# The second group's recurrence of a hybrid decoder step: 64-token chunks and one shared function

## The chip, the cores and the metric

The kernel runs on one core of one Trainium2 chip. The metric is device microseconds of one execution. TensorE (PE) multiplies, VectorE (DVE), ScalarE (ACT) and GpSimd (POOL) do elementwise work, SyncE (SP) issues transfers. Each engine works through its own queue in order and waits on semaphores for the others.

## What is computed

Two layers of a hybrid decoder step over 1024 prompt tokens and 8 single-token decodes. A layer projects the normalized input once, and from that feeds an HGRN2 group (6 heads, key width 64), a GLA group (6 heads, key width 32, value width 64) and an S5 group, each with a gate; an output projection follows. HGRN2 and GLA share one recurrence with a decay for each key channel:

```
S_t = diag(a_t) S_{t-1} + k_t v_t^T ;  o_t = S_t^T q_t
```

computed by chunks of tokens:

```python
b = jnp.cumsum(gc, axis=1)
o_inter = jnp.einsum('bthk,bhkv->bthv', qc * jnp.exp(b), S)
...
att = jnp.einsum('bthk,bshk,btshk->bths', qc, kc, decay)
o_intra = jnp.einsum('bths,bshv->bthv', att, vc)
...
S_new = jnp.exp(b_last)[..., None] * S + jnp.einsum(
    'bshk,bshv->bhkv', kc * jnp.exp(b_last[:, None] - b), vc)
```

The chunk's length is free: any length gives the same outputs up to rounding.

## The kernel before

All is fp32. The trunk of a layer is its in-projection: 25 weight tiles of 128 columns, each multiplied with 1032 tokens. Weights and activations are split into a high and a low part, and three products are summed into the PSUM tile ps_g; these matmuls of 384 or 264 columns are called gemms here (line 156 is the helper that issues every matmul). A tile's result is evicted by DVE at line 737. Between gemms the kernel advances Python generators, its "threads": one for S5, one for each unit of the recurrences, for the decodes and the gates. tick() moves every thread one yield further, twice per 24 gemms. So a yield places what follows it some gemms later in the program, and a scheduler then fixes the in-order queue of each engine. A lock lets one recurrence run at a time; need() waits for free slots in SBUF. PSUM has two banks each for ps_g, for ps_o and for ps_aux, and ps_att spans two.

A unit of the HGRN2 group, called A below (unit_a, five lines up to 1100), takes two heads of width 64, which fill 128 partitions; there are three in a layer. A tile of the GLA group, called B (unit_b, lines 1103 to 1202), takes heads of width 32: four in the first tile (128 partitions), two in the second (64). Two heads make one unit of output, so B has three such units in a layer too. Both go through the same steps:

- decay (line 867): running sums of the log decay, one DVE scan for each chunk, then their middle value is taken off. A has chunks of 64 tokens, 16 scans; B of 128, 8 scans.
- transposes of the keys into ktm (A) or ktmB (B), by PE, evicted by ACT.
- factors (line 886): GpSimd writes a chunk's decay to every state column in the tile Sp.
- kv: k^T v of each chunk on PE into ps_aux; DVE multiplies by the decay (line 1032 in A, twice; 1144 in B, once).
- states (line 891): one DVE scan along Sp and the products (in the tile onorm) makes the state of every chunk.
- att: keys by queries into ps_att. A's small matmul is 64 by 64, B's 128 by 128 with 32 rows for the contraction.
- mask: DVE copies the part below the diagonal into the zeroed tiles atts (line 1064 with maskA, line 1166 with maskB).
- inter: state by query into ps_o; intra: masked block by value, summed into the same bank.
- headnorm (lines 893 to 910): normalizes ps_o into onorm; sl is its subtraction at line 901, two PE matmuls follow.

In A the masks of a unit are bound to stand behind its inter matmuls ("behind", line 1064), one yield before intra, and a unit covers all 1024 tokens with two ps_o banks. In B a unit goes in two halves of 512 tokens; a half's inter and intra stand together, and the next half's query-key product and masks are issued behind them, ahead of headnorm.

Of the kernel before, what the change touches and what calls it, by code (L numbers as in the profile page):

```python
# [14 lines left out]
P = 128  # L15
# [23 lines left out]
def tile_hybrid_step(ctx: ExitStack, tc: tile.TileContext, a: dict, nl=NL, limit=RANGE):  # L39
# [105 lines left out]
    def act(out, in_, func, **kw):  # L145
        return S.activation(out=out, in_=in_, func=func, **kw)  # L146
# [20 lines left out]
    maskB = cst.tile([P, P], I8, name="maskB")  # L167
# [487 lines left out]
    def layer(l, slow=False):  # L655
# [296 lines left out]


# [8 lines left out]
        def unit_a(j, s1, s2, qs):  # L962
# [41 lines left out]
            kt, qt = s2, qs  # L1004
            yield from core_lock.take()
            yield from need(1)
            ktm = alloc("ktm", [P, 8, P])
            for h in range(2):
                p = psum("aux")
                for i in range(4):  # L1010
                    t0 = 512 * h + P * i
                    TE.transpose(out=p[:, i * P:(i + 1) * P], in_=kt[:, t0:t0 + P], identity=ident)
                act(out=ktm[:, 4 * h:4 * h + 4, :].rearrange("p a b -> p (a b)"), in_=p, func=AF.Copy)
                yield
            Sp = tmp("Sp", [P, 1024])
            factors(Sp, ac, 16)
            S3 = Sp.rearrange("p (v c) -> p c v", c=16)
            yield from need(1)
            on = alloc("onorm", [P, NT])
            po = None  # L1020
            asb = {}

            def kv():
                p = [psum("aux").rearrange("p (c v) -> p c v", v=64) for _ in range(2)]
                for c in range(16):
                    pr_, par = divmod(c, 2)
                    for h in range(2):
                        mm(p[par][64 * h:64 * h + 64, pr_, :], ktm[64 * par:64 * par + 64, pr_, 64 * h:64 * h + 64],
                           vA[64 * par:64 * par + 64, pr_, (2 * j + h) * 64:(2 * j + h) * 64 + 64])
                x = on[:, :T].rearrange("p (v k r) -> p r k v", k=8, r=2)  # L1030
                for par in range(2):
                    V.tensor_tensor(out=x[:, par], in0=p[par], in1=ac.rearrange("p (k r) -> p r k", r=2)[:, par]
                                    .unsqueeze(2).to_broadcast([P, 8, 64]), op=ALU.mult)
                states(Sp, on, 16)


            da = [x.rearrange("p a b c -> p (a b c)").rearrange("p (h a t) -> p h a t", h=2, t=64) for x in atts]

            def att():
                p = psum("att", (P, 2, 512))  # L1040
                for pair in range(8):
                    for par in range(2):
                        t0 = (2 * pair + par) * 64
                        for h in range(2):
                            mm(p[64 * par:64 * par + 64, h, pair * 64:pair * 64 + 64], kt[64 * h:64 * h + 64, t0:t0 + 64],
                               qt[64 * h:64 * h + 64, t0:t0 + 64])
                return p

            def inter(po):

                for pair in range(8):
                    for par in range(2):
                        c = 2 * pair + par
                        for h in range(2):
                            ph = slice(64 * h, 64 * h + 64)
                            if c:
                                x = mm(po[par][ph, pair * 64:pair * 64 + 64], S3[ph, c - 1, :], qt[ph, c * 64:c * 64 + 64],
                                       start=(pair == 1 - par), stop=False)
                                if pair == 7:
                                    yield x  # L1060

            def mask(p, done):
                for i, d in enumerate(da):
                    x = V.copy_predicated(out=d, mask=maskA.unsqueeze(1).unsqueeze(1).to_broadcast([P, 2, 4, 64]),
                                          data=p[:, :, 256 * i:256 * i + 256].rearrange("p h (a t) -> p h a t", t=64))
                    behind(x, done)

            def intra(po):

                for pair in range(8):  # L1070
                    for par in range(2):
                        r = slice(64 * par, 64 * par + 64)
                        for h in range(2):
                            mm(po[par][64 * h:64 * h + 64, pair * 64:pair * 64 + 64],
                               vA[r, pair, (2 * j + h) * 64:(2 * j + h) * 64 + 64], da[pair // 4][r, h, pair % 4, :],
                               start=False, stop=(pair == 7))

            if j == 0:
                for x in atts:
                    G.memset(x, 0.0)  # L1080
            kv()
            p = att()
            yield
            yield
            onorm[j] = on
            po = [psum("o") for _ in range(2)]
            mask(p, list(inter(po)))
            release(ktm)
            sfin = tmp("sfin", [P, 64], bufs=2)
            G.tensor_copy(out=sfin, in_=S3[:, 15])  # L1090
            SY.dma_start(out=a["hg_p"][l, :, j], in_=sfin)
            yield
            intra(po)
            release(kt)
            release(qt)
            x = on[:, :T].rearrange("p (c r t) -> p r c t", r=2, t=64)
            for par in range(2):
                yield from headnorm(po[par], x[:, par], 64)
                yield
            core_lock.give()  # L1100


        def unit_b(ti, s, q, k):
# [12 lines left out]
            ac = yield from decay(s[:, :T], s[:, :T], pr, P, 1.0 / 16.0)  # L1116
# [7 lines left out]
            yield from core_lock.take()  # L1124
            yield from need(1)
            ktm = alloc("ktmB", [P, 8, pr])
            for h in range(2):
                p = psum("aux")
                for i in range(4):
                    t0 = 512 * h + P * i  # L1130
                    TE.transpose(out=p[:, i * pr:(i + 1) * pr], in_=k[:pr, t0:t0 + P], identity=ident[:pr, :pr])
                act(out=ktm[:, 4 * h:4 * h + 4, :].rearrange("p a b -> p (a b)"), in_=p[:, :4 * pr], func=AF.Copy)
                yield
            Sp = tmp("Sp", [P, 1024])[:pr]
            factors(Sp, ac, 8)
            S3 = Sp[:, :512].rearrange("p (v c) -> p c v", c=8)
            yield from need(1)
            on = alloc("onorm", [P, NT])
            p = psum("aux").rearrange("p (c v) -> p c v", v=64)
            for c in range(8):  # L1140
                for h in range(nh):
                    mm(p[32 * h:32 * h + 32, c, :], ktm[:, c, 32 * h:32 * h + 32],
                       vB[:, c, (h0 + h) * 64:(h0 + h) * 64 + 64])
# [471 lines left out]
```

## Time and profile before

| | before |
|---|---|
| runs, us | 1102.15, 1095.07, 1093.75 (median 1095.07) |
| profiled execution, us | 1096.44 |
| its span, us | 1094.5 |
| mean granted clock of TensorE | 0.963 of full speed |
| PE busy | 1023.2 us, 8071 instructions |
| DVE busy | 696.4 us |
| ACT, POOL busy | 483.7 us, 463.7 us |

The span runs from the first to the last instruction of the core. One fp32 matmul of the program appears as two instructions in the trace. Small matmuls on different parts of the array overlap, so a group's mean duration says little of its cost: the busy time divided by the count does, as overlap is counted once in it. Idle time of an engine is given with what ended it.

### The profile page before, as it was taken

The numbers are of one execution on the slowest core, as the hardware profiler recorded it, in microseconds if no ns is written. First come the engines' busy times: TensorE is split into PE (matmuls) and PEld (weight loads), VectorE is DVE, ScalarE is ACT, GpSimd is POOL, SyncE is SP. The second block draws the span as 40 slices with busy tenths as digits, with TensorE's granted clock in tenths as the row PEclk, the third lists the DMA queues.
The fourth block names the chain that finished last, engine by engine and source line by source line (L and its number), as shares of the span: only waits on it lengthen the run. The fifth ranks groups of instructions, "written<-read, shape, count | busy, mean of one in ns | idle before, by whom it ended". The sixth has DMA issues, their size and how long they took to land.

```text
span 1094.5 us, 21166 instructions
## 1 busy us (share of the span) xinstructions
PE 1023.2 (93%) x8071; PEld 956.4 (87%) x8071; DVE 696.4 (64%) x1591; ACT 483.7 (44%) x996; POOL 463.7 (42%) x619
## 2 busy tenths in 40 slices
PE   6899999999989899999999998999998999999992
PEld 5789977789889789999999987878997889999992
DVE  8996844955776798544574574482468685652344
ACT  8233223355533646643332412334553555763431
POOL 4536673413553644522172277340244253561323
PEclk8999969999989899999999999999998989999996
DMA  7131112211112021144414113111111112112314
GB/s 226 55 99 51 42 55 76 61 51 40 61 36 61 29 89 40 39 143 129 124 53 127 48 38 98 52 48 50 29 54 47 56 39 80 39 57 87 100 53 145
DMA packets 78812, 76.78 MB, mean 70 GB/s; under 512 B 24524, under 2 KB 60652, under 8 KB 78700
## 3 DMA queue, kind: packets, MB, share of 16 engines
q1 hardware_dynamic: 78700, 75.33, 22.8%
q8 instruction: 65, 1.06, 0.4%
q14 instruction: 47, 0.39, 0.1%
HBM read 58.01 MB, written 15.53 MB: 67 GB/s over the span
## 4 chain that ended last, share of the span: by engine, by line
PE 60%; DVE 21%; POOL 6%; issue 3%; DMA 3%; ACT 3%; SPq 2%; DVEq 0%; POOLq 0%; ACTq 0%
PE ps_g L156 47%; PE ps_aux L156 7%; PE ps_o L156 4%; PE ps_att L156 1%; DMA x<-in_xT 1%; DVE wl L289 1%; DVE ep L867 1%; DVE sB L867 1%; DVE s5W L581 1%; DVE sl L901 1%; DVE Sp L891 1%; SPq L638 1%; ACT ep L146 1%; DVE flags L337 1%; PE ps_aux L846 1%
## 5 line engine op out<-in xcount | busy, mean ns | idle before, releaser
L156 PE MATMUL ps_g<-hh,wh 128*128 128x384 f32 (+1 forms) x1168 | 386.4, 331 | 9.1 <-DVE z L737 3.0
L156 PE MATMUL ps_g<-hh,wl 128*128 128x384 f32 (+1 forms) x1168 | 384.0, 329 | 2.0 <-POOL wl L289 1.5
L156 PE MATMUL ps_g<-lo,wh 128*128 128x384 f32 (+1 forms) x1168 | 382.3, 327 | 0.0
L156 PEld LDWEIGHTS ps_g<-hh,wh 128*128 128x128 f32 x1168 | 224.9, 193 | 15.8 <-DVE z L737 3.8
L156 PEld LDWEIGHTS ps_g<-hh,wl 128*128 128x128 f32 x1168 | 224.1, 192 | 6.8 <-POOL wl L289 2.2
L156 PEld LDWEIGHTS ps_g<-lo,wh 128*128 128x128 f32 x1168 | 224.8, 192 | 2.8 <-issue 0.6
L289 POOL TENSOR_TENSOR wl<-raw,wh 128x256 fp32r<-128x256 f32 x127 | 108.3, 854 | 255.5 <-ACT wh L146 219.2
L146 ACT ACTIVATE wh<-raw 128x256 fp32r<-128x256 f32 x258 | 102.4, 411 | 123.4 <-PE ps_g L156 106.2
L156 PE MATMUL ps_g<-m,wh 128*128 128x384 f32 (+1 forms) x567 | 136.2, 320 | 0.0
L289 DVE TENSOR_TENSOR wl<-raw,wh 128x256 fp32r<-128x256 f32 x131 | 77.6, 592 | 41.0 <-ACT wh L146 32.9
L156 PEld LDWEIGHTS ps_g<-m,wh 128*128 128x128 f32 x567 | 99.0, 188 | 0.4
L156 PE MATMUL ps_g<-m,wl 128*128 128x384 f32 (+1 forms) x261 | 83.4, 319 | 0.0
L1333 POOL TENSOR_TENSOR z<-z,sg 128x384 f32<-128x384 f32 (+1 forms) x48 | 48.5, 1011 | 50.9 <-ACT sg L146 40.1
L156 PEld LDWEIGHTS ps_g<-m,wl 128*128 128x128 f32 x261 | 49.1, 188 | 0.2
L146 ACT ACTIVATE sg<-z 128x384 f32<-128x384 f32 (+1 forms) x48 | 23.4, 487 | 35.9 <-DVE z L1331 30.5
L1343 DVE SCALAR_TENSOR_TENSOR onorm<-z,vec,onorm 128x384 f32<-128x384 f32 (+1 forms) x36 | 23.4, 650 | 20.6 <-POOL z L1333 20.6
L156 PE MATMUL ps_g<-vx,wh 128*128 128x384 f32 (+1 forms) x129 | 34.0, 321 | 0.0
L737 DVE TENSOR_TENSOR z<-ps_g,rn 128x384 f32<-128x384 f32 (+1 forms) x48 | 24.4, 507 | 14.0 <-PE ps_g L156 14.0
L146 ACT ACTIVATE sg<-sg 128x384 f32<-128x384 f32 (+2 forms) x56 | 31.8, 568 | 3.2 <-DVE sg L774 2.2
L146 ACT ACTIVATE sg<-sg,ones 128x384 f32<-128x384 f32 (+2 forms) x52 | 32.3, 622 | 0.9
L1422 DVE TENSOR_TENSOR ext<-ps_g,ext 128x384 f32<-128x384 f32 (+1 forms) x24 | 12.3, 512 | 31.9 <-PE ps_g L156 31.9
L1422 DVE TENSOR_TENSOR lo<-ps_g,ext 128x384 f32<-128x384 f32 (+1 forms) x24 | 12.3, 512 | 30.7 <-PE ps_g L156 30.6
(404 smaller groups left out, 1926.7 us busy)
## 6 DMA issues: line engine op xcount, KB each, us to landing
raw<-in_wf SPq DMA_DIRECT2D x100, 256.0 KB, 2.8
raw<-in_wo SPq DMA_DIRECT2D x32, 256.0 KB, 2.8
x<-in_xT SPq DMA_DIRECT2D x16, 192.0 KB, 4.7
ext<-in_xT SPq DMA_DIRECT2D x16, 192.0 KB, 2.4
x1d<-ext SPq DMA_DIRECT2D x16, 192.0 KB, 2.2
ext<-x1d SPq DMA_DIRECT2D x16, 192.0 KB, 3.2
usd<-ucp SPq DMA_DIRECT2D x4, 512.0 KB, 3.3
s5U<-usd SPq DMA_DIRECT2D x32, 64.0 KB, 2.4
```

Of the source, the lines that this page charges most:

```text
L146: return S.activation(out=out, in_=in_, func=func, **kw)
L156: return TE.matmul(out=out, lhsT=lhsT, rhs=rhs, start=start, stop=stop)
L289: e.tensor_tensor(out=wl, in0=r, in1=wh.bitcast(F32), op=ALU.subtract)
L337: V.tensor_reduce(out=flags[:p0, c:c + 1], in_=x2d, axis=mybir.AxisListType.X, op=ALU.min)
L581: V.tensor_tensor_scan(out=W_[:, ri, q], data0=m8[:, q0 + q:q0 + q + 1].to_broadcast([P, P]), data1=W_[:, ri, q], initial=0.0, op0=ALU.mul ...
L638: SY.dma_start(out=yk[16 * g:16 * g + 16, :T].rearrange("p (t k) -> p t k", t=8), in_=ysd[:, :, g, :].rearrange("t c k -> c t k"))
L737: V.tensor_tensor(out=dst[:, o:o + n], in0=p, in1=rn[:, o:o + n], op=ALU.mult)
L846: TE.transpose(out=p[:, c * P:(c + 1) * P], in_=f[:, t0:t0 + P], identity=ident)
L867: V.tensor_tensor_scan(out=g[:, cs], data0=zero[:pr].to_broadcast([pr, ch]) if plus is None else plus[:, cs], data1=x[:, cs], initial=0.0, ...
L1333: G.tensor_tensor(out=z[:, c], in0=z[:, c], in1=sg[:, c], op=ALU.mult)
L1343: V.scalar_tensor_tensor(out=on[:, c], in0=z[:, c], scalar=g, in1=on[:, c], op0=ALU.mult, op1=ALU.mult)
L1422: V.tensor_tensor(out=x, in0=p, in1=xo, op=ALU.add)
```

## The change

unit_a's recurrence becomes a function, recurrence(pr, kd, kt, qt, ac, vt, h0, fin_out, units), which both groups call: pr partitions, heads of width kd, and a list of the units of two heads that share one kv and one states step. B calls it with kd = 32 and with decays over 64 tokens. So B's chunks are 64 tokens: 16 for a head. A chunk's query-key block is 64 by 64, so the masked blocks of a head cover half the area, and the masks of a unit are two, with maskA, where they were four with maskB. maskB goes, with its load, and so do GpSimd's four memsets of atts (line 1080). Each of B's units now covers 1024 tokens, and its order is A's: query-key, yield, inter and masks behind it, yield, intra, headnorm of either bank with yields.

```diff
-    maskB = cst.tile([P, P], I8, name="maskB")
...
+        def recurrence(pr, kd, kt, qt, ac, vt, h0, fin_out, units):
...
+            Sp = tmp("Sp", [P, 1024])[:pr]
+            factors(Sp, ac, 16)
...
+            def kv():
+                p = [psum("aux").rearrange("p (c v) -> p c v", v=64) for _ in range(2)]
+                for c in range(16):
+                    pair, par = divmod(c, 2)
+                    for h in range(nh):
+                        mm(p[par][kd * h:kd * h + kd, pair, :], ktm[64 * par:64 * par + 64, pair, kd * h:kd * h + kd],
+                           val(par, pair, h))
...
+                states(Sp, on[:pr], 16)
...
+            def att(u):
+                p = psum("att", (P, 2, 512))
+                for pair in range(8):
+                    for par in range(2):
+                        t0 = (2 * pair + par) * 64
+                        for h in range(2):
+                            r = slice((2 * u + h) * kd, (2 * u + h + 1) * kd)
+                            mm(p[64 * par:64 * par + 64, h, pair * 64:pair * 64 + 64], kt[r, t0:t0 + 64], qt[r, t0:t0 + 64])
...
+            kv()
+            p = att(0)
+            yield
+            yield
+            for u, unit in enumerate(units):
+                if u:
+                    yield from need(1)
+                    on = alloc("onorm", [P, NT])
+                    p = att(u)
+                    yield
+                onorm[unit] = on
+                po = [psum("o") for _ in range(2)]
+                mask(p, list(inter(u, po)))
...
+                yield
+                intra(u, po)
...
+                for par in range(2):
+                    yield from headnorm(po[par], x[:, par], 64)
+                    yield
+            core_lock.give()
...
-            if j == 0:
-                for x in atts:
-                    G.memset(x, 0.0)
...
+            yield from recurrence(P, 64, s2, qs, ac, vA, 2 * j, a["hg_p"][l, :, j], [j])
...
-            ac = yield from decay(s[:, :T], s[:, :T], pr, P, 1.0 / 16.0)
+            ac = yield from decay(s[:, :T], s[:, :T], pr, 64, 1.0 / 16.0)
...
+            yield from recurrence(pr, 32, k, q, ac, vB, h0, a[f"gl_p{ti}"][l], [3 + 2 * ti + hp for hp in range(nh // 2)])
...
-        for i, m in enumerate((maskA, maskB, maskD)):
+        for i, m in ((0, maskA), (2, maskD)):
```

The change also moves instructions in the queues. Three places follow.

PE in layer 0 at B's second tile, between its kv (ps_aux from v and ktmB) and its inter (ps_o from qk and Sp); s5V, s5O, s5U and s5T are S5's, ident marks a transpose. Before:

```order
910 L156 MATMUL ps_aux_2494<-v_849,ktmB_2417 32x64 x16
...
924 L156 MATMUL ps_att_2635<-qk_213_1668,kb_214_1669 128x128 x3
925 L156 MATMUL ps_aux_2531<-s5V_2043,s5O_2437 128x136 x2
...
929 L846 MATMUL ps_aux_2557<-ident,vf_2216 128x128 x4
930 L156 MATMUL ps_o_2620<-qk_213_1668,Sp_2490 64x128 x6
```

In the left-out rows stand ten further S5 matmuls and nine gemms. After, at the same place, where wg, yh and yl belong to S5's gate:

```order
1068 L156 MATMUL ps_aux_2723<-v_845,ktm_2643 32x64 x16
1069 L156 MATMUL ps_aux_2724<-v_845,ktm_2643 32x64 x16
1070 L850 MATMUL ps_aux_2793<-ident,vf_2295 8x128
1071 L156 MATMUL ps_aux_2850<-yh_2828,wg_2815 128x384
1072 L156 MATMUL ps_aux_2850<-yl_2829,wg_2815 128x384
...
1077 L156 MATMUL ps_o_2859<-qk_212_1664,Sp_2719 64x64 x2
```

The left-out rows are four more matmuls of the gate. The S5 matmuls and the gemms between kv and inter are gone from this place, and the query-key product stands ahead of kv now (rows 967 to 969, not shown).

DVE in layer 0 at the second unit of B's first tile: its masks (line 1166 before, 1013 after) and S5's block (sd to the scans s5W). Before:

```order
397 L1166 COPY_PREDICATED atts_92<-maskB,ps_att_2158 128x512
398 L1166 COPY_PREDICATED atts_93<-maskB,ps_att_2158 128x512
399 L901 TENSOR_TENSOR sl_2171<-sq_2169,sh_2170 128x512
400 L568 COPY sd_751<-s5V_2043 128x64
401 L571 TENSOR_TENSOR t_83_752<-s5V_2043,s5E_1547 128x512
402 L586 COPY s5V_2043<-x_43_275 128x8x8
403 L592 TENSOR_TENSOR so_282<-so_282,sd_751 128x2x32
404 L910 TENSOR_TENSOR onorm_1884<-ps_o_2141,sq_2210 128x512
405 L575 TENSOR_TENSOR t_83_752<-s5V_2043,s5E_1547 128x512
406 L581 SCALAR_TENSOR_TENSOR s5W_2232<-sm_274,s5W_2232 128x128 x3
407 L1166 COPY_PREDICATED atts_92<-maskB,ps_att_2252 128x512
```

After:

```order
400 L567 COPY sd_747<-s5V_2145 128x64
401 L570 TENSOR_TENSOR t_82_748<-s5V_2145,s5E_1543 128x512
402 L585 COPY s5V_2145<-x_42_271 128x8x8
403 L591 TENSOR_TENSOR so_278<-so_278,sd_747 128x2x32
404 L909 TENSOR_TENSOR onorm_1888<-ps_o_2078,sq_2290 128x8x64
405 L574 TENSOR_TENSOR t_82_748<-s5V_2145,s5E_1543 128x512
406 L580 SCALAR_TENSOR_TENSOR s5W_2311<-sm_270,s5W_2311 128x128 x4
407 L584 MEMSET s5V_2145 128x8
...
412 L580 SCALAR_TENSOR_TENSOR s5W_2311<-sm_270,s5W_2311 128x128 x4
413 L1013 COPY_PREDICATED atts_91<-maskA,ps_att_2317 128x512
414 L1013 COPY_PREDICATED atts_92<-maskA,ps_att_2317 128x512
```

In the left-out rows stand short instructions of S5. Before, one pair of masks stands ahead of the block and one inside it, behind three of the scans; after, the pair stands behind both rows of four scans.

DVE in layer 0 at the first unit of A, around the two multiplications of its kv (line 1032 before, 981 after) and its states scan (891, 890). Before:

```order
557 L1032 TENSOR_TENSOR onorm_3242<-ps_aux_3245,ac_3138 128x8x64
558 L1032 TENSOR_TENSOR onorm_3242<-ps_aux_3246,ac_3138 128x8x64
559 L891 SCALAR_TENSOR_TENSOR Sp_3239<-Sp_3239,onorm_3242 128x1024
560 L988 COPY q_510_3543<-qs_3044 128x8
561 L867 SCALAR_TENSOR_TENSOR ep_3530<-zero,s_438_3042 128x64 x16
```

After:

```order
553 L1090 COPY q_508_3740<-qs_3243 128x8
554 L866 SCALAR_TENSOR_TENSOR ep_3727<-zero,s_436_3241 128x64 x16
555 L981 TENSOR_TENSOR onorm_3441<-ps_aux_3442,ac_3337 128x8x64
556 L873 TENSOR_SCALAR bm_3806<-ep_3727 128x16
557 L981 TENSOR_TENSOR onorm_3441<-ps_aux_3443,ac_3337 128x8x64
558 L874 TENSOR_TENSOR ac_3807<-bm_3806 128x16
559 L336 TENSOR_REDUCE flags<-bm_3806 128x1
560 L876 TENSOR_TENSOR ep_3727<-ep_3727,bm_3806 128x1024
561 L890 SCALAR_TENSOR_TENSOR Sp_3438<-Sp_3438,onorm_3441 128x1024
```

The 16 scans at line 866 are the decay of the next unit of A; they stand ahead of the multiplications now, and before the change they stood behind the states scan.

## Rows read from the trace of the kernel before

**Rows 1.** The page: busy us and instructions, the granted clock, the last chain by engine.

```profile
PE 1023.2 (93%) x8071; PEld 956.4 (87%) x8071; DVE 696.4 (64%) x1591; ACT 483.7 (44%) x996; POOL 463.7 (42%) x619
...
PEclk8999969999989899999999999999998989999996
...
PE 60%; DVE 21%; POOL 6%; issue 3%; DMA 3%; ACT 3%; SPq 2%; DVEq 0%; POOLq 0%; ACTq 0%
```

**Rows 2.** Groups by shape, PE, of B: instructions | busy us, mean ns | idle before.

```profile
L156 PE MATMUL ps_o<-atts,v 128*64 128x128 f32 x192 | 16.9, 283 | 0.3 <-DVE atts L1166 0.3
...
L156 PE MATMUL ps_att<-qb,kb 32*128 32x128 f32 x128 | 11.9, 306 | 0.0
...
L156 PE MATMUL ps_o<-qb,Sp 32*64 32x128 f32 x112 | 9.2, 295 | 0.0
...
L156 PE MATMUL ps_att<-qk,kb 32*128 32x128 f32 x64 | 6.8, 296 | 0.0
...
L156 PE MATMUL ps_o<-qk,Sp 32*64 32x128 f32 x56 | 5.5, 302 | 0.0
...
L156 PE MATMUL ps_aux<-v,ktmB 128*32 128x64 f32 x192 | 4.6, 221 | 0.1
```

**Rows 3.** The same view, PE, of A.

```profile
L156 PE MATMUL ps_o<-qs,Sp 64*64 64x64 f32 x360 | 23.2, 287 | 6.1 <-DVE Sp L891 3.1 <-DVE f L985 3.0
...
L156 PE MATMUL ps_aux<-v,ktm 64*64 64x64 f32 x384 | 10.4, 223 | 1.1 <-ACT ktm L146 1.1
...
L156 PE MATMUL ps_att<-qs,s 64*64 64x64 f32 x384 | 8.7, 223 | 0.0
...
L156 PE MATMUL ps_o<-atts,v 64*64 64x64 f32 x384 | 7.1, 222 | 1.9 <-DVE atts L1064 1.9
```

**Rows 4.** Groups by shape, DVE.

```profile
L1166 DVE COPY_PREDICATED atts<-maskB,ps_att 128x512 f32<-128x512 int8 x24 | 16.1, 725 | 7.1 <-PE ps_att L156 4.2 <-PE ps_o L156 2.9
...
L891 DVE TENSOR_TENSOR_SCAN Sp<-Sp,onorm 128x1024 f32<-128x1024 f32 x6 | 16.1, 2686 | 0.2
...
L867 DVE TENSOR_TENSOR_SCAN ep<-zero,s 128x64 f32<-128x64 f32 x48 | 11.2, 310 | 0.0
...
L891 DVE TENSOR_TENSOR_SCAN Sp<-Sp,onorm 128x512 f32<-128x512 f32 x2 | 2.4, 1206 | 0.0
```

**Rows 5.** Windows at half clock: us, PE busy (instructions), granted clock; six in A, one in B.

```profile
306.80:310.00 3.20, 3.20 (x25) 0.51 0.45 116
...
361.40:368.00 6.60, 6.34 (x20) 0.50 0.06 20
...
sum 29.30, PE 28.53; mean PE 4.75
...
139.65:156.40 16.75, 16.65 (x73) 0.50 0.06 18
```

**Rows 6.** Timeline, PE, layer 0: start, us, operation, idle before and its releaser.

```profile
138.30 0.50 PE L156 MATMUL ps_aux<-s5V,s5O 64*128 64x136 f32 x4 [1.94 <-POOL s5O L603]
```

**Rows 7.** Timeline, layer 0, the first A unit from kv to inter.

```profile
299.42 1.94 DVE L1032 TENSOR_TENSOR onorm<-ps_aux,ac 128x512 f32<-128x512 f32 x2
...
301.46 2.29 DVE L891 TENSOR_TENSOR_SCAN Sp<-Sp,onorm 128x1024 f32<-128x1024 f32 x1
301.51 0.34 PE L156 MATMUL ps_g<-lo,wh 128*128 128x384 f32 x1
...
301.69 0.33 PE L156 MATMUL ps_g<-hh,wl 128*128 128x384 f32 x1
...
303.81 0.88 PE L156 MATMUL ps_o<-qs,Sp 64*64 64x64 f32 x12 [1.44 <-DVE Sp L891]
```

**Rows 8.** Timeline, DVE, layer 0: S5's block in front of a mask.

```profile
190.28 0.19 DVE L568 COPY sd<-s5V 128x64 f32<-128x64 f32 x1
...
191.41 4.38 DVE L586 COPY s5V<-x 128x64 f32<-128x64 f32 x1
...
198.35 2.07 DVE L581 TENSOR_TENSOR_SCAN s5W<-sm,s5W 128x128 f32<-128x128 f32 x3
```

More of the change, by code (lines that the diff above doesn't have):

```diff
@@ L1003, in unit_a @@
             yield
[L1004 to L1034, printed above, removed]
@@ L1037, in unit_a @@
[L1037 to L1060, printed above, removed]
@@ L1062, in mask @@
[L1062 to L1076, printed above, removed]
@@ L1078, in unit_a @@
-            if j == 0:
-                for x in atts:
-                    G.memset(x, 0.0)
[L1081 to L1100, printed above, removed]
+            yield from recurrence(P, 64, s2, qs, ac, vA, 2 * j, a["hg_p"][l, :, j], [j])
         def unit_b(ti, s, q, k):
@@ L1123, in unit_b @@
             yield
[L1124 to L1143, printed above, removed]
@@ L1144, in unit_b @@
-            V.tensor_tensor(out=on[:pr, :512].rearrange("p (v c) -> p c v", c=8), in0=p[:pr],
-                            in1=ac[:, :8].unsqueeze(2).to_broadcast([pr, 8, 64]), op=ALU.mult)
-            states(Sp, on[:pr], 8)
-            sfin = tmp("sfin", [P, 64], bufs=2)[:pr]
-            G.tensor_copy(out=sfin, in_=S3[:, 7])
-            SY.dma_start(out=a[f"gl_p{ti}"][l], in_=sfin)
-            release(ktm)
-            yield
-            seq = [(hp, hf) for hp in range(nh // 2) for hf in range(2)]
@@ L1154, in att @@
-            def att(hp, hf):
-                p = psum("att", (P, 2, 512))
-                for cc in range(4):
-                    t0 = (4 * hf + cc) * P
-                    for g in range(2):
-                        r0 = 32 * (2 * hp + g)
-                        mm(p[:, g, cc * P:cc * P + P], k[r0:r0 + 32, t0:t0 + P], q[r0:r0 + 32, t0:t0 + P])
-                return p
-            def mask(p):
-                for i, d in enumerate(atts):
-                    V.copy_predicated(out=d, mask=maskB.unsqueeze(1).unsqueeze(1).to_broadcast([P, 2, 2, P]),
-                                      data=p[:, :, 256 * i:256 * i + 256].rearrange("p h (a t) -> p h a t", a=2))
@@ L1185, in unit_b @@
-            mask(att(*seq[0]))
-            yield
-            for i, (hp, hf) in enumerate(seq):
-                if hf == 0:
-                    if hp:
-                        yield from need(1)
-                        on = alloc("onorm", [P, NT])
-                    onorm[3 + 2 * ti + hp] = on
-                yield
-                po = psum("o")
-                outputs(hp, hf, po)
-                if i + 1 < len(seq):
-                    mask(att(*seq[i + 1]))
-                else:
-                    release(q)
-                    release(k)
-                yield from headnorm(po, on[:, 512 * hf:512 * hf + 512])
@@ L1202, in unit_b @@
-            core_lock.give()
+            yield from recurrence(pr, 32, k, q, ac, vB, h0, a[f"gl_p{ti}"][l], [3 + 2 * ti + hp for hp in range(nh // 2)])
         def scan_pair(f, q, k, r0, kd, head, sel, u, sfin):
```

67 lines of the change are left out of this document (53 added, 14 removed).

## The prediction

> **What bounds the kernel now.** I read the page first. TensorE's matmuls are busy for 1023.2 of 1094.5 us, and the chain that ended last runs through PE for 60% and through DVE for 21% of the span [rows 1]. So a change pays if it takes time from PE's queue or a wait out of it. Work added on DVE costs nothing except where PE stands behind it. The row of the granted clock has slices of 8 and 9 tenths: PE also loses time by running at half clock.
>
> Then I read PE's groups with shapes kept apart. The GLA recurrence (B, six head pairs in two layers) has six groups [rows 2]: kv 4.6 us, query-key 11.9 + 6.8, inter 9.2 + 5.5, intra 16.9; together 54.9 us. The HGRN2 recurrence (A, also six head pairs) is the shape that B gets [rows 3]: kv 10.4, query-key 8.7, inter 23.2, intra 7.1; together 49.4 us. In front of A's inter PE idles 6.1 us, in front of its intra 1.9, in front of kv 1.1; in front of B's intra 0.3 [rows 2, 3]. B as it is hardly makes PE wait, A does. That is the question of this case.
>
> Third, the windows by granted clock. Six stretches in A's part of the two layers, 29.3 us together, ran at 0.50 to 0.53, the lower level, 1.2 GHz; another of 16.75 us lies in the middle of B's first units [rows 5]. The first stretch of A follows a stop of PE before inter, the B one a stop of 1.94 us for S5's s5O [rows 6, 7]. Of a PE-bound stretch at half clock half is lost: 14.6 us in A's six, 8.4 us in B's.
>
> **The change on PE.** Six head pairs of B get the instruction counts of A's six: kv 192 to 384 instructions, query-key 192 to 384, inter 168 to 360, intra 192 to 384 (one fp32 matmul shows as two). Priced by A's rows this is 49.4 − 54.9 = −5.5 us: kv +5.8, query-key −10.0, inter +8.5, intra −9.8. The two products of the masked block gain, since half of their area was above the diagonal; the two with the state lose, since there are twice as many states.
>
> A's tiles have 64 rows for the contraction, B's have 32. In the new code, heads take two row groups and the chunk's parity two column halves, so four small matmuls stand side by side, as in A; that is why I take A's price of 8.7/384 = 23 ns for an instruction. The other bound is B's own row: 18.7/192 = 97 ns at 128 columns, 49 at 64 if the time goes by columns alone, times 384 = 18.7 us, no gain on query-key and +10.0 to the sum. The lower bound is A's row itself: nothing in the trace is cheaper.
>
> The Trainium skill, page "TensorEngine Tiling (Array Packing)", section Instruction Overhead, speaks against the change: each matmul has about 60 cycles of overhead, and no factor should be taken from a dimension that is already small. For the 768 added instructions that is, as an estimate by that page at 2.4 GHz, 25 ns each: 19 us one behind the other, 4.8 us with four side by side, which would leave 0.7 of the 5.5 us. The trace bears it out only in part: A's instruction at 64 columns takes 23 ns with its overhead in it [rows 3].
>
> **The change on DVE and GpSimd.** Masks: 24 of 725 ns become 12 of the same size, half of 16.1 us gone; their removal takes no PE time, as PE waited 0.3 us for them [rows 2, 4]. A tile's decay has 16 scans instead of 8; 48 of A's take 11.2 us, so 16 take 3.7. The states scan doubles from 1.2 to between 2.3 and 2.7 us, four times: +4.4 to +5.9; the kv multiplication comes twice instead of once a tile, 0.97 each, +3.9 [rows 4, 7]. DVE's total moves by a few us and is no bound. GpSimd's four memsets of the masked tiles and SyncE's one mask load go; PE does not stand behind either, so nothing is taken for them. The wider GpSimd copy that spreads the decay into Sp lies between the transposes and kv and is done under gemms.
>
> **New waits of PE.** The second part of the cost is where DVE's chain (two multiplications 1.94 us, states scan 2.29 [rows 7]: 4.2 us) has too little PE work beside it. A gemm of 384 columns takes 0.175 us at full clock, from one start to the next [rows 7].
> - Layer 0, second tile: after the change kv is followed by one short transpose and six gemms of S5's gate, 1.1 us, and then inter (first order piece). 4.2 − 1.1 = a wait of 3.1 us; before, nine gemms, twelve S5 matmuls and the query-key product stood there. If the yl subtraction ahead of it on DVE is late too, up to 4.3. I take 3.1.
> - Layer 0, first tile: 26 gemms, 4.5 us, against 4.2 and a short eviction that I put at most at one multiplication's 0.97: 0 to 0.7, I take 0.3.
> - Layer 0, first tile's second unit: its two masks now stand on DVE behind S5's block and eight s5W scans (second piece). In the trace of before, that block takes 8.1 us from the sd copy to the first scan, 4.38 of them in one copy; then eight scans at 0.69 = 5.5, and a mask 0.7: 14.3 us [rows 4, 8]. On PE 29 gemms (5.1 us), 23 inter matmuls (46 instructions at 23.2/360: 3.0) and some 18 small ones, about 1.5, stand between: 9.6. The wait is 4.7 us if the subtraction of headnorm that PE needs at the start of this stretch is done just in time, and 0 if it is done 4.7 earlier. I take the middle, 2.4.
> - Layer 1: 27 and 29 gemms (4.7 and 5.1 us) cover the 4.2; I take 0.
> - Clock: a stop of 1.44 us in A was followed by 3.2 us at half clock [rows 5, 7], that is 1.6 us lost. Two such new stops: +3.2 (0 if the clock holds, 6.6 if they are as long as A's longest of 6.6 us).
>
> **A's units, moved but not changed.** B's recurrence takes more steps, so A's stands later against the gemms. In layer 0 the first A unit gets 32 gemms (5.6 us) between kv and inter, but DVE has the next unit's 16 decay scans in front of its chain (third piece): 3.7 + 1.94 + 2.29 and a subtraction of 128x1024, which I put at a states scan, 2.3: 10.2 us, a wait of up to 4.6 where it was 1.44 [rows 7]. If the scans are done before kv ends, it goes. Lower end −1.4 − 1.6 of clock = −3; upper end +3.2 and one more stretch, +4.8. The value lies near neither end: I take 0.
>
> **Sum.** −5.5 + 3.1 + 0.3 + 2.4 + 3.2 + 0 = +3.5 us on the profiled execution's 1096.44; that lies 1.4 above the median of the three runs, 1095.07, so I forecast 1095.1 + 3.5 = 1098.6 us. All low ends, with the half clock in B's part gone: −5.5 + 3.1 − 3 − 8.4 = −13.8, 1081. All high ends: +4.5 + 4.3 + 0.7 + 4.7 + 6.6 + 4.8 = +25.6, 1121.
>
> **Rivals.**
> 1. Faster. The 16.75 us at half clock start with PE stopped for S5's s5O [rows 5, 6]; B's first unit stands beside that. If the new order gives PE something to do there, 8.4 us come back, and if DVE runs ahead the new waits stay near 1: −5.5 − 8.4 + 1 = −12.9, 1082. For it: B's masks leave DVE and the masked products no longer run at half clock. Against: s5O's lateness is GpSimd's, which the change hardly touches. Chance 0.2.
> 2. Slower. B takes over all of A's stalls, not just the shape: A's six pairs show 6.1 + 1.9 + 1.1 us of waits before their own matmuls and 14.6 lost to clock, 23.7 us. In B: −5.5 + 23.7 = +18.2, 1113. Place: every kv to inter and inter to intra of B. It decides when the stalls pass 16.5 us, two thirds of A's. Against: in layer 1 the order leaves 27 gemms and more beside the chain, and part of A's half clock follows headnorm waits at the end of its row of units. Chance 0.18.
> 3. The small tiles do not pay (32 rows, twice the instructions): query-key stays at 18.7, the sum is +4.5 + 9.0 = +13.5, 1108.6. The tiling page's rule would be the reason. For it: B's 97 ns for an instruction; against: A's 23. Chance 0.1.
>
> **Numbers.** My own case, 1098.6 with a range of 1090 to 1106, has 0.52. One per cent, 11 us, is about what a measurement of this kernel can tell from no change. Rival 1 is the faster side, 0.2. Rival 2 and most of rival 3 are the slower side, 0.25. The rest, 0.55, lies within 1%. The range that holds 8 in 10 goes from 1084, inside rival 1, to 1111, between rivals 3 and 2.
>
> **What would show it.** PE's kv, query-key, inter and intra groups of B near 10.4, 8.7, 23.2 and 7.1 us (step one); a wait of PE for the states scan of some 3 us in the second tile of layer 0, and one for the masks of the second unit (step two); a stretch at half clock behind each; no such wait in layer 1; A's waits about as before. The prediction is wrong if query-key stays above 14 us, if the 16.75-us stretch is gone, or if B's waits come in layer 1 too.

## The result and the profile after

The changed kernel takes 1124.9 us (median; 1124.35 to 1127.96), the kernel before 1094.4 beside it: 1.0275 times, with a 95% interval of 1.0216 to 1.0334. The forecast was 1098.6 us with a range of 1084 to 1111. The profiled execution took 1124.35 us, its span is 1122.5, the mean granted clock 0.951 (before: 1094.5 and 0.963).

The page of the changed kernel, busy time by engine and the granted clock in 40 slices:

```profile
PE 1031.3 (92%) x8839; PEld 969.9 (86%) x8839; DVE 698.0 (62%) x1614; ACT 494.1 (44%) x1005; POOL 458.1 (41%) x615
...
PEclk9999978998998899999999999999898999999997
```

Against [rows 1], DVE has the same time. PE has 8 us more and the span 28 us more, so PE stands still 20 us longer (1122.5 − 1031.3 = 91.2 us against 71.3).

PE's groups in the changed kernel with shapes kept apart, as in [rows 2, 3]; qb and qk are B, qs is A; the intra row (atts) holds both groups:

```profile
L156 PE MATMUL ps_o<-qb,Sp 32*64 32x64 f32 x240 | 17.1, 278 | 0.0
L156 PE MATMUL ps_o<-atts,v 64*64 64x64 f32 x768 | 15.5, 229 | 4.6 <-DVE atts L1013 4.5
...
L156 PE MATMUL ps_o<-qk,Sp 32*64 32x64 f32 x120 | 7.6, 282 | 1.2 <-DVE Sp L890 1.2
...
L156 PE MATMUL ps_att<-qb,kb 32*64 32x64 f32 x256 | 6.9, 237 | 0.0
...
L156 PE MATMUL ps_aux<-v,ktm 64*32 64x64 f32 x384 | 6.7, 223 | 0.0
...
L156 PE MATMUL ps_att<-qk,kb 32*64 32x64 f32 x128 | 3.7, 250 | 0.0
```

B's kv is 6.7 us, query-key 10.6, inter 24.7, intra 15.5 less A's 7.1 = 8.4: 50.4 us in place of 54.9. PE's own work did fall.

What PE waited for in the changed kernel (engine, line, what it waited for: us in total, times, longest):

```profile
PE ps_aux L156 <- ACT sh L146: 15.3, 8, 4.5
PE ps_aux L156 <- POOL s5O L602: 6.7, 2, 4.1
...
PE ps_att L156 <- DVE qs L1102: 4.9, 2, 2.5
...
PE ps_o L156 <- DVE atts L1013: 4.5, 3, 2.4
...
PE ps_o L156 <- DVE Sp L890: 2.0, 2, 1.2
```

The longest total, 15.3 us, belongs to headnorm: its first PE matmul waits for ScalarE's square and rounding (sh). The line of the kernel before for it is this:

```profile
PE ps_aux L156 <- ACT sh L146: 3.5, 2, 2.0
```

Windows of the changed kernel in B's part of the two layers that ran at half clock (us, PE busy, granted clock):

```profile
186.00:193.00 7.00, 7.00 (x56) 0.51 0.11 16
220.00:228.00 8.00, 7.61 (x37) 0.57 0.19 62
254.00:262.00 8.00, 7.94 (x65) 0.57 0.11 33
752.00:763.00 11.00, 9.00 (x47) 0.54 0.11 26
790.00:794.00 4.00, 4.00 (x23) 0.57 0.01 3
800.00:804.00 4.00, 4.00 (x34) 0.57 0.00 0
sum 42.00, PE 39.55; mean PE 6.59
```

The stretch of [rows 5] at 139 us is there as before; these six are B's too, 42 us of windows in a part that ran at full clock in the kernel before but for one short stretch (716 to 720 us). At the clocks shown they cost 18.8 us. Four of them (220, 254, 752 and 790 us) begin in a stop of PE or at most 3 us behind one, as all stretches of the kernel before in its recurrences do; those at 186 and 800 us, 5.2 us of the cost, begin with no stop of 0.35 us or more in the 10 us ahead of them. The first follows inter's 60 instructions. The PE timeline there (start, us, operation):

```profile
183.27 1.54 PE L156 MATMUL ps_o<-qb,Sp 32*64 32x64 f32 x22
184.74 0.33 PE L942 MATMUL ps_aux<-ident,dV 128*128 128x128 f32 x1
185.00 2.46 PE L156 MATMUL ps_o<-qb,Sp 32*64 32x64 f32 x38
187.38 2.08 PE L156 MATMUL ps_aux<-s5U,s5Bm 128*64 128x136 f32 x16
189.40 0.59 PE L156 MATMUL ps_g<-hh,wh 128*128 128x264 f32 x1
189.78 0.42 PE L156 MATMUL ps_g<-lo,wh 128*128 128x264 f32 x1
```

**One sum for every kernel.** A span is PE's work at full clock, plus its stops (span − busy), plus what half clock costs. A stretch of granted clock c loses 1 − c of its time, so the cost is (1 − mean clock) × span; it is counted as if PE were busy in all of it. Before: 982.7 + 71.3 + 40.5 = 1094.5. After: 976.3 + 91.2 + 55.0 = 1122.5. So: work −6.4, stops +19.9, clock +14.5, sum +28.0.

Two limits of this sum. First, half clock costs no work where PE stands still at it. Counted in windows of 1 us and for PE's busy part alone, the clock costs 31.5 us before and 44.4 after, and the work is 991.7 and 986.8: clock +12.9, work −4.9. The work column below is therefore good to some 10 us only: by it the six 64-token kernels with the same matmuls differ by 10.8 us, by the second count by 6. Second, it is the sum of one execution. The granted clock is on record for each: by (1 − mean clock) × span the four executions of the changed kernel lost 55.0 to 61.8 us (median 60.2, the profiled one is the lowest), the 60 of the kernel before beside the experiments 29.4 to 50.6 (median about 41). By these medians the change lost some 19 us by the clock and some 11 by work and stops together.

The same sum for all experiments (medians of each against the kernel before on its chip; work, stops and clock from the profiled execution; the last column is the granted clock between 180 and 270 us, where B stands in layer 0):

| kernel | B's chunk | median us | times before (95%) | work | stops | clock cost | clock 180 to 270 |
|---|---|---|---|---|---|---|---|
| before | 128 | 1094 to 1098 | 1 | 982.7 | 71.3 | 40.5 | 1.00 |
| changed | 64 | 1124.9 | 1.0275 (1.0216 to 1.0334) | 976.3 | 91.2 | 55.0 | 0.89 |
| k1_ahead64 | 64 | 1131.2 | 1.0325 (1.0255 to 1.0395) | 969.8 | 96.4 | 65.6 | 0.87 |
| k2_behind128 | 128 | 1105.3 | 1.0093 (1.0058 to 1.0129) | 980.9 | 78.8 | 44.2 | 0.98 |
| k3_split | 64 | 1110.2 | 1.0143 (1.0101 to 1.0186) | 972.7 | 74.9 | 56.3 | 0.79 |
| k4_copy | 64 | 1125.4 | 1.0260 (1.0204 to 1.0316) | 946.0 | 108.9 | 70.9 | 0.83 |
| k5_small | 128, small matmuls | 1128.9 | 1.0357 (1.0278 to 1.0436) | 1002.2 | 64.7 | 58.5 | 0.83 |
| k6_dve | 128 | 1096.1 | 0.9993 (0.9973 to 1.0014) | 980.2 | 71.9 | 41.6 | 0.98 |
| k7_both | 128, small matmuls | 1146.0 | 1.0456 (1.0403 to 1.0508) | 1004.7 | 72.4 | 65.1 | 0.83 |
| k8_late | 128 | 1097.6 | 1.0009 (0.9988 to 1.0029) | 983.9 | 68.2 | 43.8 | 1.00 |
| k9_nointer | 64, no inter | 1099.8 | 1.0041 (1.0018 to 1.0064) | 957.5 | 91.6 | 48.3 | 0.96 |
| k10_inter | 128, small inter | 1103.5 | 1.0069 (1.0044 to 1.0094) | 995.4 | 65.2 | 36.2 | 0.94 |
| k11_shift2 | 64 | 1120.1 | 1.0237 (1.0190 to 1.0285) | 976.5 | 72.3 | 68.1 | 0.87 |
| k12_shift5 | 64 | 1142.2 | 1.0416 (1.0372 to 1.0461) | 967.0 | 97.1 | 76.4 | 0.81 |
| k13_beforecopy | 128 | 1101.8 | 1.0050 (1.0029 to 1.0071) | 975.3 | 83.0 | 42.9 | 1.00 |
| k14_copyyield | 64 | 1125.3 | 1.0271 (1.0218 to 1.0325) | 949.5 | 102.3 | 70.7 | 0.85 |
| k15_yield | 64 | 1112.7 | 1.0155 (1.0108 to 1.0202) | 977.8 | 73.8 | 57.7 | 0.89 |

The median of k5_small is without one execution of 1144.9 us, which ran at a lower clock (0.930).

### The profile page after: what moved, and what is told of

Read it like the earlier page. It is cut to its first block, busy times and chain, and to the rows that moved or that the text cites. A ratio compares the mean times of both kernels' runs of the same rounds, so it can differ in the third digit from the quotient of the medians.

```text
span 1122.5 us, 22692 instructions
## 1 busy us (share of the span) xinstructions
PE 1031.3 (92%) x8839; PEld 969.9 (86%) x8839; DVE 698.0 (62%) x1614; ACT 494.1 (44%) x1005; POOL 458.1 (41%) x615
## 3 DMA queue, kind: packets, MB, share of 16 engines
q8 instruction: 71, 1.16, 0.4%
## 5 line engine op out<-in xcount | busy, mean ns | idle before, releaser
L156 PEld LDWEIGHTS ps_g<-hh,wh 128*128 128x128 f32 x1168 | 228.1, 195 | 20.6 <-issue 4.7
L156 PEld LDWEIGHTS ps_g<-hh,wl 128*128 128x128 f32 x1168 | 227.4, 195 | 9.4 <-DVE wl L288 3.0
L156 PEld LDWEIGHTS ps_g<-lo,wh 128*128 128x128 f32 x1168 | 228.0, 195 | 2.8 <-issue 0.6
L288 POOL TENSOR_TENSOR wl<-raw,wh 128x256 fp32r<-128x256 f32 x127 | 105.1, 829 | 268.0 <-ACT wh L146 237.6
L288 DVE TENSOR_TENSOR wl<-raw,wh 128x256 fp32r<-128x256 f32 x131 | 73.1, 558 | 39.6 <-ACT wh L146 31.8
L1261 POOL TENSOR_TENSOR z<-z,sg 128x384 f32<-128x384 f32 (+1 forms) x48 | 47.7, 997 | 50.6 <-ACT sg L146 37.1
L1271 DVE SCALAR_TENSOR_TENSOR onorm<-z,vec,onorm 128x384 f32<-128x384 f32 (+1 forms) x36 | 26.4, 737 | 26.3 <-POOL z L1261 26.2
L909 DVE TENSOR_TENSOR onorm<-ps_o,sq 128x512 f32<-128x512 f32 x24 | 16.5, 688 | 32.3 <-ACT sq L146 32.1
L1350 DVE TENSOR_TENSOR ext<-ps_g,ext 128x384 f32<-128x384 f32 (+1 forms) x24 | 12.3, 512 | 32.0 <-PE ps_g L156 32.0
```

Of the source, the lines that this page charges most:

```text
L156: return TE.matmul(out=out, lhsT=lhsT, rhs=rhs, start=start, stop=stop)
L288: e.tensor_tensor(out=wl, in0=r, in1=wh.bitcast(F32), op=ALU.subtract)
L909: V.tensor_tensor(out=dst if n < 512 else run(dst), in0=run(po), in1=run(rs), op=ALU.mult)
L1261: G.tensor_tensor(out=z[:, c], in0=z[:, c], in1=sg[:, c], op=ALU.mult)
L1271: V.scalar_tensor_tensor(out=on[:, c], in0=z[:, c], scalar=g, in1=on[:, c], op0=ALU.mult, op1=ALU.mult)
L1350: V.tensor_tensor(out=x, in0=p, in1=xo, op=ALU.add)
```

## The experiments

The theories after the result. "Order": B took over A's order of steps, and PE stands behind DVE and ScalarE there. "Chunk", later "small matmuls": PE's clock falls because B is now twice as many matmuls of half the size. "DVE": the longer scans of 64-token chunks. "Moved": A's units come later.

**Is it the order of steps?** The changed kernel with the order of before in B, and the kernel before with A's order in B:

```diff
# k1_ahead64, B only
+                mask(att(0), [])
...
+                    list(inter(u, po))
+                    intra(u, po)
+                    if u + 1 < len(units):
+                        mask(att(u + 1), [])
...
# k2_behind128
+                p = att(hp, hf)
...
+                mask(p, inter(hp, hf, po))
+                yield
+                intra(hp, hf, po)
```

> The changed kernel (64-token chunks in B), but B's units go in the order of the kernel before: the masks right behind the query-key product and ahead of inter, inter and intra in one piece, the next unit's query-key product and masks ahead of headnorm. Theory 'order' (the time went into the step order of A that B took over: PE stands behind DVE and ACT at masks and headnorm, and runs at half clock after each stop): 1103 to 1112 us, B's half-clock stretches of 6.8 us at the first tile gone. Theory 'chunk' (the 64-token chunks cost it themselves, since inter is a run of 60 small matmuls with few gemms around it): stays at 1120 to 1128. Theory 'moved' (mainly A's units, which come later): 1115 to 1125.

> The kernel before with its 128-token chunks in B, but with A's order of steps in B: query-key, yield, inter, masks behind inter, yield, intra, headnorm, yield, for each half of a unit. Theory 'order': 1106 to 1118 us, with new waits of PE for masks and headnorm in B. Theory 'chunk': 1092 to 1098. Theory 'moved': 1100 to 1110, since B takes even more steps and A comes later.

The old order does not bring the time back: k1 takes 1131.2 us, above what any theory expected, and B's part of layer 0 runs at 0.87. A's order costs the 128-token kernel some 10 us, 7.5 of them stops; that is just below what "order" expected and within "moved". So the order explains a part at most, and "order" as the main cause falls.

**Is it inter's run?** One step in the middle of B's inter:

```diff
-                mask(p, list(inter(u, po)))
+                    list(inter(u, po, range(4)))
+                    yield
+                    mask(p, list(inter(u, po, range(4, 8))))
```

> The changed kernel, B's inter in two halves of 30 instructions with one yield (12 gemms) between. Theory 'chunk': the half clock that begins without a stop of PE, at 186 and at 800 us in the changed kernel, goes, 1116 to 1121 us. Theory 'order': 1123 to 1129, waits and half clock as in the changed kernel. Theory 'moved': 1125 to 1130, A comes later by three more steps in a layer.

1110.2 us, better than any theory had it, but not for the expected reason: the half clock behind the first unit's inter is still there, and the clock's cost is 56.3 us. What went is stops, 91.2 to 74.9.

**Is it the strided weights of inter?** ScalarE copies the states once, so that a chunk's 64 values lie together:

```diff
+                act(out=C3, in_=S3, func=AF.Copy)
...
-                                x = mm(..., S3[r, c - 1, :],
+                                x = mm(..., C3[r, c - 1, :],
```

> The changed kernel, the states copied once by ScalarE (1.1 us) so that inter's weights are contiguous, in both groups. If the strided weights set inter's price (23.2 us for 360 instructions against 8.7 us for 384 of query-key), inter of A and B falls from 47.7 to some 20 us. Theory 'chunk': with it half-clock stretches behind inter go too, 1085 to 1098 us. Theory 'order': PE waits 1 to 2 us longer for each of the ten states, the clock stretches stay, 1100 to 1112.

Inter fell, from 47.7 us in both groups to 16.3 + 10.3 + 6.9 = 33.5, and PE's busy time with it by 14.4 us (by the second count above the work fell by 22 us; the 30 of the table count half clock at which PE stood still). Nothing came of it: stops rose to 108.9 us, and the clock cost to 70.9. A copy takes 2.0 us, not the 1.1 expected, and lies on the way from states to inter: PE waits 18.6 us for copies and 10.7 for masks. So the stride sets a good part of inter's price; the time does not follow.

**PE's small matmuls, DVE's work, or the delay, each alone in the kernel before:**

```diff
# k5_small: query-key, and inter in the same way
+                        for e in (0, 64):
+                            mm(p[:, g, cc * P + e:cc * P + e + 64], k[r0:r0 + 32, t0:t0 + P], q[r0:r0 + 32, t0 + e:t0 + e + 64])
# k6_dve: two scans of 64 for one of 128, kv product and states scan twice
+                for c0 in range(c * ch, c * ch + ch, 64):
...
+            for o in (512, 0):
...
# k8_late: behind the last unit of a tile
+            yield from pause(3 if ti == 0 else 2)
```

> The kernel before (128-token chunks), B's query-key and inter matmuls each issued as two of 64 columns: PE gets the instruction counts of the changed kernel there (384 and 336), nothing else changes. Theory 'small matmuls' (PE's clock falls because B's work is a run of small instructions): half clock of 10 us or more between 180 and 270 us, 1108 to 1118 us. Theory 'DVE': no half clock there; inter +8 us by A's row and query-key about the same, 1098 to 1104.

> The kernel before, PE's work unchanged, with DVE's work of 64-token chunks in B: every decay scan of 128 as two of 64 (the second starts from the first's end), the kv multiplication and the states scan each issued twice, the extra one ahead of the real one into spare columns. Theory 'DVE' (longer blocks on DVE make PE wait, and the clock falls behind the waits): 1105 to 1115 us, half clock between 180 and 270 us. Theory 'small matmuls': 1094 to 1098.

> Both of it, the small matmuls and the longer DVE work, in the order and with the 128-token chunks of the kernel before. If the two explain the loss: 1115 to 1128 us; if the loss is in the step order and in where A's units land: 1100 to 1106.

> The kernel before, B's lock held three steps longer in the first tile and two in the second, with no work in them: A's units start later, as in the changed kernel, and all else is as before. Theory 'moved' (A's units find fewer gemms beside them or DVE busier): 1102 to 1112 us, A's waits up by 6 us or more in a layer. Otherwise 1093 to 1098.

DVE's work and the delay cost nothing: 0.9993 and 1.0009, both intervals around 1. The small matmuls alone cost some 3%, more than either theory expected. The view that settles the clock is this one, windows of k5_small (us, PE busy, granted clock):

```profile
198.00:209.00 11.00, 11.00 (x83) 0.53 0.12 32
229.00:250.00 21.00, 21.00 (x104) 0.51 0.10 27
sum 32.00, PE 32.00; mean PE 16.00
```

PE does not stop in these 32 us, nor for 0.35 us or more anywhere between 180 and 300 us; the total of its stops, 64.7, is below that of the kernel before. And yet it is at half clock. Query-key in k5_small, to be held against [rows 2]:

```profile
L156 PE MATMUL ps_att<-qb,kb 32*128 32x64 f32 x256 | 23.9, 316 | 0.0
...
L156 PE MATMUL ps_att<-qk,kb 32*128 32x64 f32 x128 | 13.8, 316 | 0.0
```

98 ns for an instruction at 64 columns, 97 at 128: with 128 columns of weights the price is by instruction, hardly by moved columns. Part of either ran at half clock, but at full clock it is much the same: 32 instructions at 64 columns in 2.05 us (k5_small, from 254.94 us), 16 at 128 in 1.16 (before, from 186.56). So k5_small adds 19 us of query-key besides the clock, and its total is not a copy of the changed kernel's. k7_both has both parts: 1146.0 us, above what either theory expected.

**Inter left out, and inter alone made small:**

```diff
# k9_nointer
-                for pair in range(8):
+                for pair in range(8 if kd == 64 else 0):
# k10_inter: inter's part of k5_small
+                            for e in (0, 64):
```

> The changed kernel with B's inter left out (the product of state and query is missing in B's outputs; the states themselves are still computed). It takes away 24.7 us of PE's busy time, the runs of 60 small matmuls and the waits for the states scan. Theory 'small runs' (such a run itself lowers the clock): the half clock at 186 and 254 us goes, 1082 to 1094 us. Theory 'stops' (the clock falls only behind waits of PE): 1096 to 1104 us, just the work.

> The kernel before with B's inter alone issued as two matmuls of 64 columns (336 instead of 168 instructions), query-key as it was. Work by A's row: +8 us. Theory 'small runs': half clock of 10 us or more between 180 and 270 us on top, 1107 to 1116 us. Theory 'stops': 1098 to 1104 us. In the run with both split, query-key had also doubled from 18.7 to 37.7 us, which blurs it.

Without B's inter (its outputs then lack that product) the clock in B's part is 0.96, and its cost is 48.3 us: of the 14.5 us that the change lost to clock, inter's matmuls carry 6.7; by the medians of all executions (50.5 against 60.2) some 10 of 19. Windows of k9_nointer, of the changed kernel and of the kernel before:

```profile
180.00:270.00 90.00, 84.23 (x910) 0.96 0.20 56
```

```profile
180.00:270.00 90.00, 82.81 (x942) 0.89 0.17 48
```

```profile
180.00:270.00 90.00, 89.44 (x698) 1.00 0.20 56
```

The time, 1099.8 us, lies where "stops" expected it, and the stops stayed (91.6); but the clock did not stay, so that theory's reason does not hold. In k10_inter the window is at 0.94. Its profiled execution, with a clock cost of 36.2 us, was one of the fastest of ten; the median of the ten is 42.9, as in the kernel before (41.5), and 1103.5 us is just the added work. So inter's small matmuls alone do not make the loss.

**Is it where A's units land?** The changed kernel with B's lock held longer, two steps a tile and five:

```diff
+            if kd == 32:
+                yield from pause(2)
             core_lock.give()
```

> The changed kernel, B's lock held two steps longer at the end of each tile, no work added: A's units land elsewhere against gemms and S5. Theory 'landing' (some 17 us of the loss lie in A's units, by where they land): 1108 to 1120 us, and A's part of a layer changes by 5 us or more. Theory 'late' (later is worse): 1126 to 1135. If A's part doesn't depend on it: 1122 to 1128.

> The same with five steps at the end of each tile. Theory 'landing': another value than with two steps, within 1105 to 1130 us and not in order with the number of steps. Theory 'late': 1130 to 1145, slower than with two steps.

1120.1 and 1142.2 us. With two steps the stops are 72.3 us, those of the kernel before; with five 97.1. In the kernel before a like delay (k8_late) did nothing. Two steps lie at the upper end of "landing" and outside "late"; five lie above what "landing" expected and within "late", but their two longest stops, 12.3 and 8.4 us, are waits of B's part for S5's gate (yh). B's own second tile is delayed in both, so A's landing is not separated from it here.

**The copy with a covering step, its control, and the copy in the kernel before.** One more yield between kv and inter; k15_yield has it alone, k13_beforecopy has step and copy for A in the kernel before:

```diff
             p = att(0)
             yield
             yield
+            yield
```

> The kernel before; in A alone the states are copied once by ScalarE so that inter's weights are contiguous, and one step more stands between kv and inter to cover the copy. A's inter falls from 23.2 to some 16 us. If the runs of strided loads and the stops are what costs clock: 1083 to 1091 us, faster than the kernel before. If where A's units land decides: 1092 to 1104.

> The changed kernel with contiguous states in both groups and one step more between kv and inter, so that the copy's wait (18 us of stops in the run without that step) is covered. Theory 'runs and stops cost the clock': inter some 33 us instead of 48, stops back under 60 us, half clock under 90 us: 1085 to 1100. Theory 'landing': anything from 1105 to 1140.

> The changed kernel with that one step more between kv and inter, no copy. It is the control to the run above. If the step alone covers the waits for states: 1112 to 1122; if the stops are elsewhere (headnorm, evictions): 1122 to 1135 or by landing.

k15_yield is the cleanest case of all: its stops (73.8) are within 2.5 us of the kernel before, its work is 4.9 us less, and it is still 1.55% slower, by a clock cost of 57.7 against 40.5 (57.7 to 68.2 in its four executions). A window of it:

```profile
752.00:773.00 21.00, 21.00 (x113) 0.51 0.09 26
```

Here a stop of 2.05 us for sh (at 750.31) comes first, and then PE works without stopping for 21 us at half clock, through S5's and B's small matmuls and headnorm. The copy fails again (k14_copyyield, 1125.3: the wait for the copy is down to 1.5 us, but ScalarE is later with ktm, 4.9 us of waits, and sh, 21.2). In the kernel before, A's inter falls from 23.2 to 15.4 us with it, and 11.8 us of stops for the copy and 8.7 for masks take more than that back. No version ran faster than the kernel before.

**Falls of the clock with and without a stop.** The traces of all runs can be sorted by what PE did before each fall of the granted clock (from 100 us on, without the last 40 us). In the kernel before, k2_behind128, k6_dve, k8_late and k13_beforecopy, in k9_nointer, and in k4_copy and k14_copyyield, all 87 falls stand in a stop of PE of 0.35 us or more, or at most 3.0 us behind its end. In the nine kernels that have B's inter in small matmuls with strided weights, 23 of 122 falls have no such stop in the 6 us before them: 2 of 14 in the changed kernel, 3 of 9 in k5_small, 3 of 16 in k15_yield. So with these matmuls in its queue PE can lose the clock while it is busy throughout; in one profile of each kernel no such fall is seen without them, or with contiguous weights. The falls behind stops remain, and in k4_copy and k14_copyyield the clock costs some 71 us even so.

## Why the prediction was wrong, step by step

**What bounds the kernel** was read rightly: DVE's added work in k6_dve cost nothing, and the loss shows as PE's stops and PE's clock.

**PE's price** held as a sum. Forecast −5.5 us; the groups show −4.5, and at full clock it is −6.4 or −4.9 by the two counts above. kv was dearer in the forecast (10.4) than in the run (6.7); its weights have 32 columns, A's 64. Query-key was cheaper there (8.7, run 10.6; A's own took 10.3 in this run). The 32-row tiles do overlap: 10.6/384 = 28 ns for an instruction that lasts some 240. Rival 3 falls. So does the estimate by the overhead that the Trainium skill, "TensorEngine Tiling (Array Packing)", section Instruction Overhead, gives: it left 0.7 of the 5.5 us, and the run shows 4.5. For another shape the trace goes further than that section: k5_small gained next to nothing from half the columns. The Trainium skill, "TensorE: Matmul & The Clock Gate", section "LDWEIGHTS (loading the stationary operand)", has the time of a weight load go by the column count; the loads in k5_small's query-key take 221 ns at 128 columns, those of A's 134 at 64, which goes the same way, though less than in proportion.

**The new waits in B** were forecast one by one, in layer 0 3.1 + 0.3 + 2.4, in layer 1 none. The second tile waits 1.2 us for the states scan (252.10 us) where 3.1 were forecast, and there is no wait for the states in the first tile or for the masks of its second unit. B's stops of 0.35 us and more in layer 0 grew by 6.3 us all the same, close to the 5.8 forecast, but that is luck: they stand elsewhere. The stop for s5O at 139 us is 4.1 us where it was 1.94 and 0.95, and a wait came that the forecast did not have. Behind that unit's intra, headnorm's square is queued on ScalarE; its timeline:

```profile
214.10 1.28 ACT L146 ACT_TABLE_LOAD   x1
215.40 2.08 ACT L146 ACTIVATE yc<-s5yk 128x1024 f32<-128x1024 f32 x2
217.38 0.21 ACT L146 ACTIVATE dq<-odec 128x24 f32<-128x24 f32 x1
217.59 1.28 ACT L146 ACT_TABLE_LOAD   x1
218.88 0.31 ACT L146 ACTIVATE sm<-sm 128x8 f32<-128x8 f32 x2
219.10 0.58 ACT L146 ACTIVATE sq<-ps_o 128x512 f32<-128x512 f32 x1
219.71 0.63 ACT L146 ACTIVATE sh<-sq 128x512 fp32r<-128x512 f32 x1
```

and PE's row that waits for it:

```profile
220.39 0.79 PE L156 MATMUL ps_aux<-sh,obd 128*128 128x512 f32 x1 [4.54 <-ACT sh L146]
```

Activations of S5 and the decodes and two table loads stand ahead of sq, 5 us. Only DVE's queue was read for B, not ScalarE's. The step that failed here is "DVE's chain has too little PE work beside it" as the whole list of waits. In layer 1 the forecast of 0 was wrong: B's stops of 0.35 us and more there, for masks, s5O, an eviction and others, are 8.9 us against 2.3.

**A's units** were put at 0 between −3 and +4.8. PE's stops of 0.35 us and more in A's part, evictions and weight splits among them, grew from 11.8 to 19.3 us in layer 0 and from 7.6 to 14.0 in layer 1, together 13.9, outside both ends. The forecast looked at one wait of one unit. k11_shift2 and k15_yield show that so many stops do not belong to the change as such: with two steps more, or one, in another place, the kernel's stops are at 72.3 and 73.8 us. In k3_split they are at 74.9, in k12_shift5 at 97.1. Which of them a schedule hits was not to be read from the rows that the prediction used.

**The clock** was the other large miss. The forecast priced half clock as what follows two new stops, 3.2 us; it was 14.5, and some 19 by the medians of all executions. Most of B's six stretches, 13.6 of 18.8 us, do stand behind a stop as the forecast had it, but there are four and not two, and they are longer; 5.2 us have no stop ahead, a case that the forecast did not have. The cost goes with the small matmuls and not with the length of the stops: in every kernel with 64-token chunks and all of B's matmuls (eight, 32 executions) it is 55.0 to 78.7 us, in those with 128-token chunks and B's matmuls as they were (five, 96 executions) 29.4 to 50.6. k15_yield, k3_split and k11_shift2 have stops like the kernel before and yet belong to the first. k5_small shows the fall with no stop at all around it. Rival 2, B taking over all of A's stalls, had the sign and the two parts, waits and clock, but as a size (+18.2) it was short, because it left A as it was and charged B only with what A had.

**Sum.** Forecast: work −5.5, stops +5.8, clock +3.2. Measured: −6.4, +19.9, +14.5. Of the miss of 24.5 us on the profiled executions, about 11 are the clock and 14 the stops; by the medians of all executions some 16 are the clock and 10 the rest. So two terms failed: the new waits, 5.8 in B and 0 in A where the stops of 0.35 us and more grew by 12.9 and 13.9 (elsewhere they fell by 4.3), and the clock, priced by the count of new stops.

**What is open.** That small matmuls lower the clock is shown; which property of them does it is not. Contiguous weights removed the falls without a stop but not the cost, and leaving inter out brought back half of it. Whether small matmuls make PE fall more often behind a stop, or keep it down longer, is not separated. Nor is it shown why the stops of the 64-token kernel depend so much on a step or two (72 to 97 us), while those of the kernel before did not move with k8_late (68.2).

## What to carry to other kernels

A product that is cut into more and smaller matmuls can lose more by PE's clock than it saves in work, even where PE hardly waits more (k15_yield: work −4.9, stops +2.5, clock +17.2): compare (1 − granted clock) × span before and after, over several executions, not busy time alone. When one unit is moved in a kernel of many threads, read the in-order queue of every engine that it uses, ScalarE's too, up to the next thing that PE waits for. And before a loss is put down to an edit, shift the same code by a step or two: here one step was worth 12 us.

## What the runs showed of the hardware

PE at half clock while busy all the time: 32.00 of 32.00 us at 0.51 to 0.53 in k5_small, 21.00 of 21.00 at 0.51 in k15_yield. The Trainium skill, "TensorE: Matmul & The Clock Gate", Part 1, gives half rate as the state of an idle or cold engine and full rate as that of a busy one. The falls behind stops agree with it; these windows go against it, as far as busy time in the profile means activity to the chip, and so does the stretch of [rows 5] once it had begun, with PE busy for 16.65 of 16.75 us. An instruction of fp32 query-key costs 97 to 98 ns with 128 columns of weights at 64 and at 128 moved columns, and 28 ns with 64 columns of weights in four parts of the array.
